# Layer 1's projections: the last two tiles' second gate cells move to the end of the query and key stage, and the stage's first tile is taken alone

## The chip, the cores and the metric

The kernel runs on one core of one Trainium2 chip. A core has a matrix engine (TensorE, PE in the profile), a vector engine (VectorE, DVE), an activation engine (ScalarE, ACT), a general engine (GpSimd, POOL) and a queue engine (SyncE, SP), which share an on-chip memory (SBUF) and the accumulator banks of TensorE (PSUM). Each engine works through its own list of instructions in order, and waits where an instruction needs something that another engine or a transfer has not yet delivered. Transfers (DMAs) are issued by an engine's queue and run beside it. The metric is the device time of one execution, in microseconds (us).

## The reference

The model is a stack of two layers over 2048 latent tokens and 256 context tokens with 1024 features each. Layer 0 is a mixture of full attention and gated linear attention; the change doesn't touch it. Layer 1 is a neighbourhood attention with 16 heads of 64 features. Cut to what matters:

```python
h  = rms_norm(x,  norm_g[1]) * (1 + scale)   + shift       # 2048 latent tokens
hc = rms_norm(cx, norm_g[1]) * (1 + c_scale) + c_shift     # 256 context tokens
q, k, v, z = jnp.split(jnp.dot(h, w_in), 4, axis=-1)       # 4 x 1024 columns, also for hc
q, k = rms_norm(heads(q), q_gain), rms_norm(heads(k), k_gain)
o = neighborhood_attention(q, k, v, k_ctx, v_ctx, rpb)     # window of 8 rows x 16 columns, and all 256 context keys
y = jnp.dot(o * silu(z), w_out)
x = x + gate * y
```

All of it is float32. The context's queries and gates are not needed in the last layer.

## The kernel before

The 2304 tokens are 18 tiles of 128: tiles 0 and 1 are the context, 2 to 17 the latent tokens. The 4096 columns of layer 1's input weights are eight blocks j of 512: 0 and 1 queries, 2 and 3 keys, 4 and 5 values, 6 and 7 gates. A "cell" (t, j) is one tile against one block. A float32 product is made as three products of split halves (high by high, high by low, low by high), so a cell is 24 matmuls of 128x512, eight steps of three (`mm3_steps`, L124 to L131). Tiles 0 and 1 have no query and gate cells.

Layer 1 has three stages.

`odd_qk` computes keys and queries, tile after tile. `cells` (L171 to L176) writes the order of the cells by hand: it takes the tiles in groups and goes through the blocks j within each group. The first two tiles form one group, the last two another, and those between are alone. `stream` (L178 to L195) turns that order into instructions. Two tiles can be held at once (`hbufs`, two buffers of `hhi` and `hlo`); once a tile's last cell is emitted, the tile two further on is prepared in its place. The preparation (`transposed`, `modulate`) loads the tile, sums its squares (ACT), scales it (DVE L328), transposes it on PE (L331, eight matmuls into `px`), evicts it through ACT with the layer's modulation, and splits it into high and low halves (DVE L343, L344). The weights of a block lie in one of four places w0 to w3, each with a high and a low half (`OD_PLACE`): blocks 2, 3, 0, 1 lie in w0, w1, w2, w3, and blocks 4, 5, 6, 7 follow in the same places. When the last cell of a block is through, the next block of its place is loaded over SP's queue (`wraw`, three buffers) and split on ACT (L106) and DVE (L383) in small steps, which `pump` hands out, one for every four steps of the matmuls.

A key or query cell is normalised per head (ACT square, DVE L1136, two small POOL operations, DVE L1139); then `fin` transposes it on PE (L1147, four matmuls), evicts it (ACT, into `oqh`, two buffers) and stores it: queries and keys over SP's queue (Q1, K1), a second arrangement of the keys over POOL's queue (K1t, L1184). `fin` of a cell is emitted while later cells run (`pend`). At the end of the stage the tiles 16 and 17 also get their first gate cells, j = 6: the gate is a tanh on ACT and a product on DVE (L1199), transposed like the others and stored to `z1` over POOL's queue (L1151).

`odd_vz` computes values and gates of all tiles, now from tile 17 down to tile 0, since tiles 16 and 17 are still held. Its first cells are written out by hand, and its gate cells go through their own transposes (L1239), an eviction into `ozt` and a store on ACT's queue (L1243). Woven between these cells runs `maxes`: for each of the 16 heads and 16 blocks of 128 queries, the maximum score that each query can meet, which needs two matmuls per block (L1273, L1280, into five banks `mx`) and reductions on DVE (L1275, L1286). `maxes` loads a key head pair (`mk`), a bias table per head (`mtab`, L1257) and the queries (`mq`, L1267) over SP's queue; POOL adds two masks to each table (L1258, L1259), ACT rearranges the queries into `mz`, whose unused halves DVE has set to zero (L1248). `weave` hands out 0.57 steps of `maxes` for each step of three matmuls, from the stage's first step, and lets a step of the cells be issued no earlier than a lag of 15 behind those maxima.

`odd_attention` follows. Its first loads (queries, keys, values, bias tables, masks, all at L111) are issued by SP's queue, and POOL adds a mask to its tables (L1370) ahead of the scores' correction on DVE (L1537).

The order in which each engine meets the instructions comes from the order of emission and from a scheduler that may take an instruction later than emitted, within its dependencies.

Of the kernel before, what the change touches and what calls it, by code (L numbers as in the profile page):

```python
# [10 lines left out]
F32 = mybir.dt.float32  # L11
# [6 lines left out]
P = 128  # L18
# [5 lines left out]
NT = T // P  # L24
NCT = CTX // P
# [63 lines left out]
class Kern:  # L89
# [79 lines left out]
                pass  # L169

    @staticmethod  # L171
    def cells(tiles, js, keep=lambda t, j: True, edge=2):

        n = len(tiles)
        groups = [tiles[:edge]] + [[t] for t in tiles[edge : n - edge]] + [tiles[n - edge :]]
        return [(t, j) for g in groups for j in js for t in g if keep(t, j)]  # L176

    def stream(self, cells, hT, cell, prep, done=None):  # L178
# [922 lines left out]
    def odd_qk(self, ws, win, hT):  # L1101
        nc = self.nc
# [6 lines left out]
        with ExitStack() as es:  # L1109
# [6 lines left out]
            pend, kt = [], {}  # L1116

            def cell(t, j):
                hi, lo = hT[t]
                wh, wl = win[j]  # L1120
                ps = self.tl(pp, [P, 8, 64], "gm", bufs=3)
                steps = self.mm3_steps(ps[:], (lambda k: hi[:, k, :], lambda k: lo[:, k, :]),
                                       (lambda k: wh[:, k, :], lambda k: wl[:, k, :]), range(KD))
                for n, _ in enumerate(steps):
                    if n == 5 and pend and (len(pend) > 1 or j == 6):
                        fin(*pend.pop(0))
                    yield
                if j == 6:
                    n = self.tl(sp, [P, 512], "onat", bufs=4)
                    self.gate(n, ps[:].rearrange("p h d -> p (h d)"))  # L1130
                    pend.append((t, j, n))
                    return
                sq = self.tl(sp, [P, 512], "osq")
                self.act(sq[:], ps[:].rearrange("p h d -> p (h d)"), AF.Square)
                ss = self.tl(sp, [P, 8], "oss", bufs=4)
                nc.vector.tensor_reduce(out=ss[:], in_=sq[:].rearrange("p (h d) -> p h d", h=8), axis=AX.X, op=ALU.add)  # L1136
                self.rpow(ss[:], ss[:], 1.0 / 64, EPS)
                n = self.tl(sp, [P, 512], "onat", bufs=4)
                nc.vector.tensor_tensor(out=n[:].rearrange("p (h d) -> p h d", h=8), in0=ps[:],  # L1139
                                        in1=ss[:].unsqueeze(2).to_broadcast([P, 8, 64]), op=ALU.mult)  # L1140
                pend.append((t, j, n))

            def fin(t, j, n):
                z = j // 2
                ps = self.tl(pp, [P, 4, P], "tp")
                for i in range(4):
                    nc.tensor.transpose(ps[:, i, :], n[:, i * P : i * P + P], self.ident[:])  # L1147
                hi = self.tl(sp, [P, 4, P], "oqh", F32R)
                if j == 6:
                    self.act(hi[:].bitcast(F32), ps[:])  # L1150
                    nc.gpsimd.dma_start(self.z1[:4, :, (t - NCT) * P : (t - NCT) * P + P].rearrange("j p t -> p j t"), hi[:].bitcast(F32))  # L1151
                    return
                self.act(hi[:], ps[:], AF.Copy, scale=qkg[:, z : z + 1])
                j0 = (j % 2) * 4
                if z == 1:
                    nc.sync.dma_start(self.K1[j0 : j0 + 4, :, t * P : t * P + P].rearrange("j p t -> p j t"), hi[:].bitcast(F32))
                if z == 0 or t < NCT:
                    lo = self.tl(sp, [P, 4, P], "oql", F32R)
                    nc.vector.scalar_tensor_tensor(out=lo[:], in0=ps[:], scalar=qkg[:, z : z + 1], in1=hi[:],
                                                   op0=ALU.mult, op1=ALU.subtract)  # L1160
                    if z == 0:
                        for part, tt in enumerate((hi, lo)):
                            nc.sync.dma_start(self.Q1[part][j0 : j0 + 4, :, (t - NCT) * P : (t - NCT) * P + P].rearrange("j p t -> p j t"),
                                              tt[:].bitcast(F32))
                    else:
                        store_k((hi, lo), j0, t * P, P)
                    return
                g, r0 = divmod(2 * (t - NCT), 8)
                if r0 == 0:
                    kt[j] = [self.tl(sp, [P, 4, 512], f"okt{j}{part}", F32R, bufs=1) for part in range(2)]  # L1170
                view = lambda x, n: x[:].rearrange("p i (r c b) -> p i r c b", r=n, c=4)
                for r in range(2):
                    oh, ol = (x[:].rearrange("p i (c b r) -> p i r c b", c=4, r=8)[:, :, r0 + r] for x in kt[j])
                    self.act(oh, view(ps, 2)[:, :, r], AF.Copy, scale=qkg[:, z : z + 1])
                    nc.vector.scalar_tensor_tensor(out=ol, in0=view(ps, 2)[:, :, r], scalar=qkg[:, z : z + 1],
                                                   in1=view(hi, 2)[:, :, r], op0=ALU.mult, op1=ALU.subtract)
                if r0 == 6:
                    store_k(kt.pop(j), j0, CTX + g * 512, 512)

            def store_k(parts, j0, o, w):  # L1180

                for u, x in enumerate(parts):
                    for i in range(2):
                        nc.gpsimd.dma_start(self.K1t[j0 : j0 + 4, i, u * 64 : u * 64 + 64, o : o + w].rearrange("j d t -> d j t"),  # L1184
                                            x[i * 64 : i * 64 + 64].bitcast(F32))

            nxt = {2: 4, 3: 5, 0: 6, 1: 7}
            done = lambda j: j in nxt and self.ahead.append(self.od_steps(win, nxt[j], ws))
            cells = self.cells(list(range(NT)), (2, 3, 0, 1), lambda t, j: j > 1 or t >= NCT)[:-8]
            cells += [(t, j) for j in (0, 1, 2, 3, 6) for t in (NT - 2, NT - 1)]  # L1190
            for _ in self.stream(cells, hT, cell, lambda t: self.prep(1, t, self.x1, pp, ("px", 2)), done):
                self.pump()
            while pend:
                fin(*pend.pop(0))
# [19 lines left out]
    def odd_vz(self, ws, win, hT):  # L1214
        nc = self.nc
        self.M1 = self.scr("M1", (16, SEQ), F32)
        NR, NC = (len(b) for b in BLOCKS["q"])
        with ExitStack() as es:
# [78 lines left out]
                        nc.gpsimd.dma_start(self.M1[h, g * 512 : g * 512 + 512].rearrange("(a c b) -> c a b", a=8, c=4),  # L1297
                                            r[4 * g : 4 * g + 4].rearrange("c (a b) -> c a b", a=8).bitcast(F32))

            cells = [(t, j) for j in (7, 4, 5) for t in (NT - 1, NT - 2)]  # L1300
            cells += self.cells(list(range(NT))[::-1], (4, 5, 6, 7), lambda t, j: j < 6 or t >= NCT)[8:]
            gemms = self.stream(cells, hT, cell, lambda t: self.reload(1, t))
            self.weave(gemms, maxes(), 0.57, 15)
# [395 lines left out]
```

## Time and profile before

| | |
|---|---|
| median of 3 runs | 3710.65 us (3707.5 to 3712.75) |
| the profiled execution's own time | 3709.59 us |
| its span, first to last instruction | 3707.8 us |
| mean granted clock of TensorE | 0.982 of full speed |
| TensorE busy | 3566.3 us, 96% |
| VectorE, ScalarE, GpSimd busy | 64%, 39%, 33% |
| query and key stage | about 2187 to 2626 us of the span |
| value and gate stage | about 2626 to 3114 us |

The profile is one execution. A row of a timeline gives an instruction's start and duration, its engine and line, the tiles it writes and reads, its shape, and in brackets how long the engine had stood idle before it and which instruction released it. A row of a window gives the length of the stretch, the busy time and number of instructions of PE, of its weight loads (PEld), DVE, ACT and POOL, the granted clock of TensorE, the share of the DMA engines' time in use, and the rate in GB/s. Matmuls are pipelined: a 128x512 matmul is shown with some 0.39 us, while the next one starts 0.23 us after it.

### The profile page before, as it was taken

How to read it: one execution, taken by the hardware profiler on the slowest of the kernel's cores; microseconds unless marked ns; L12 is line 12 of the kernel's file. 1: busy time of each engine (PE TensorE's matmuls, PEld its weight loads, DVE VectorE, ACT ScalarE, POOL GpSimd, SP SyncE). 2: the span in 40 equal slices, each digit the busy share in tenths (PEclk: the TensorE clock that was granted, in tenths of full speed). 3: DMA queues.
4: the chain of work that ended last, by engine and by line, in shares of the span. 5: the costliest groups of instructions: out<-in, count | busy, mean ns of one | idle time of the engine just before them, and what ended most of it. 6: DMA issues, size and time to landing. Idle time of an engine off the chain costs nothing.

```text
span 3707.8 us, 51752 instructions
## 1 busy us (share of the span) xinstructions
PE 3566.3 (96%) x18404; PEld 2754.6 (74%) x18404; DVE 2374.2 (64%) x4860; ACT 1438.5 (39%) x2741; POOL 1209.2 (33%) x1336
## 2 busy tenths in 40 slices
PE   7999989999999999999999999999899999999889
PEld 6988988888886666655656878888688887555567
DVE  4677656888876666697665344545478773666722
ACT  5545541111115555555553124444322223555400
POOL 1433420111111212122201233333344443777743
PEclk9999999999999999999999999999999999999999
DMA  7455453222242232334514543445744437887564
GB/s 257 138 164 160 129 170 98 87 75 85 75 127 63 82 97 79 91 105 121 163 55 151 165 149 117 150 142 175 215 143 123 136 117 200 216 215 205 162 195 130
DMA packets 364372, 512.18 MB, mean 138 GB/s; under 512 B 25826, under 2 KB 243890, under 8 KB 358211
## 3 DMA queue, kind: packets, MB, share of 16 engines
q1 hardware_dynamic: 322642, 425.49, 39.0%
q0 software_dynamic: 19872, 55.92, 5.1%
q10 hardware_dynamic: 21600, 27.46, 2.1%
q8 instruction: 146, 2.39, 0.3%
q14 instruction: 112, 0.91, 0.1%
HBM read 329.38 MB, written 179.37 MB: 137 GB/s over the span
## 4 chain that ended last, share of the span: by engine, by line
PE 79%; DVE 7%; DMA 6%; POOL 3%; ACT 3%; issue 2%; SPq 0%; POOLq 0%; ACTq 0%; DVEq 0%
PE gm L129 9%; PE gm L130 9%; PE gm L131 9%; PE av L905 7%; PE st L963 4%; PE mx L651 4%; PE st L964 3%; PE st L965 3%; PE pj L129 3%; PE pj L130 3%; PE pj L131 3%; PE o L1406 2%; PE st L1373 1%; DMA wraw<-w_od 1%; PE mx L1280 1%
## 5 line engine op out<-in xcount | busy, mean ns | idle before, releaser
L954 DVE TENSOR_TENSOR acc<-acc,apt 128x512 f32<-128x512 f32 x512 | 364.6, 737 | 158.3 <-ACT apt L106 155.4
L106 ACT ACTIVATE apt<-st 128x512 f32<-128x512 f32 (+1 forms) x592 | 344.4, 594 | 284.3 <-PE st L965 247.2
L652 DVE TENSOR_REDUCE mm<-mx 128x1 f32<-128x512 f32 (+1 forms) x656 | 389.3, 629 | 81.3 <-PE mx L651 74.4
L905 PE MATMUL av<-apt,av 128*64 128x512 f32 (+1 forms) x1184 | 288.0, 600 | 0.0
L963 PE MATMUL st<-aq,akh 97*128 97x512 f32 (+1 forms) x592 | 254.0, 429 | 5.1 <-ACT apt L106 2.8
L651 PE MATMUL mx<-mk,mq 96*128 96x512 f32 (+1 forms) x656 | 236.8, 373 | 6.1 <-DMA mq<-QT 4.6
L964 PE MATMUL st<-aq,akh 96*128 96x512 f32 (+1 forms) x592 | 235.2, 397 | 0.0
L965 PE MATMUL st<-aq,akl 96*128 96x512 f32 (+1 forms) x592 | 234.0, 396 | 0.0
L1286 DVE CUSTOM_DVE_ANT_1 mx<-mx,mtab 128x225 f32<-128x225 f32 (+12 forms) x576 | 183.7, 339 | 58.1 <-PE mx L1280 42.7
L106 ACT ACTIVATE u<-gm 128x352 f32<-128x352 f32 (+1 forms) x140 | 68.6, 497 | 369.4 <-PE gm L131 208.0
L905 PEld LDWEIGHTS av<-apt,av 128*64 128x64 f32 x1184 | 82.1, 138 | 157.1 <-issue 155.8
L1537 DVE TENSOR_TENSOR opt<-st,tab 128x64 f32<-128x64 f32 (+10 forms) x576 | 142.7, 316 | 86.6 <-PE st L1374 58.3
L963 PEld LDWEIGHTS st<-aq,akh 97*128 97x128 f32 x592 | 112.3, 190 | 98.4 <-issue 43.7
L1412 POOL TENSOR_TENSOR oacc<-oacc,opt 128x682 f32<-128x682 f32 (+9 forms) x144 | 169.6, 1206 | 23.2 <-ACT opt L106 21.9
L1073 POOL TENSOR_TENSOR px<-py,px 128x512 f32<-128x512 f32 x64 | 86.4, 1350 | 232.8 <-DVE py L1072 232.8
L106 ACT ACTIVATE opt<-opt 128x930 f32<-128x930 f32 (+8 forms) x130 | 104.4, 805 | 106.2 <-DVE opt L1537 102.3
L106 ACT ACTIVATE prh<-pr 128x1024 fp32r<-128x1024 f32 x32 | 33.9, 1058 | 263.1 <-PE pj L130 235.6
L651 PEld LDWEIGHTS mx<-mk,mq 96*128 96x128 f32 x656 | 121.7, 189 | 17.6 <-issue 5.0
L965 PEld LDWEIGHTS st<-aq,akl 96*128 96x128 f32 x592 | 113.6, 192 | 25.5
L964 PEld LDWEIGHTS st<-aq,akh 96*128 96x128 f32 x592 | 113.9, 192 | 18.0
L1373 PE MATMUL st<-q,kt 128*128 128x480 f32 (+5 forms) x256 | 99.0, 389 | 25.8 <-DVE opt L1537 20.9
L106 ACT ACTIVATE x<-px,modB,modA 128x128 f32<-128x128 f32 x272 | 99.3, 469 | 57.2 <-PE px L331 50.9
(517 smaller groups left out, 10069.0 us busy)
## 6 DMA issues: line engine op xcount, KB each, us to landing
q<-Q SPq DMA_DIRECT2D x48, 512.0 KB
H<-x ACTq DMA_DIRECT2D x36, 512.0 KB
adaw<-ada_w SPq DMA_DIRECT2D x64, 256.0 KB
x<-H SPq DMA_DIRECT2D x32, 512.0 KB
pr<-RT SPq DMA_DIRECT2D x32, 512.0 KB
wraw<-w_od SPq DMA_DIRECT2D x64, 256.0 KB
K1t<-okt POOLq DMA_DIRECT2D x32, 512.0 KB, 7.6
kt<-K1t SPq DMA_DIRECT2D x32, 512.0 KB
```

The source lines that it names most:

```text
L106: return self.nc.scalar.activation(out, in_, func, **kw)
L129: self.nc.tensor.matmul(out, lh(k), rh(k), start=j == 0, stop=False)
L130: self.nc.tensor.matmul(out, lh(k), rl(k), start=False, stop=False)
L131: yield self.nc.tensor.matmul(out, ll(k), rh(k), start=False, stop=j == n - 1)
L651: mm = nc.tensor.matmul(ps[:, :w], q[:A_QK, (t % 6) * P : (t % 6) * P + P], k[:A_QK, k0 : k0 + w], start=True, stop=True)
L652: nc.vector.tensor_reduce(out=m[:, t, n : n + 1], in_=ps[:, :w], axis=AX.X, op=ALU.max)
L905: nc.tensor.matmul(O[j, nb][i * 64 : i * 64 + 64, :w], V[j, kt // TT][:, kt % TT, i * 64 : i * 64 + 64], pts[i][:, :w], start=n == 0, stop ...
L954: nc.vector.tensor_tensor(out=acc[i][:, :w], in0=a[:, :w], in1=pts[i][:, :w], op=ALU.add)
L963: nc.tensor.matmul(ps[:, :w], kh[: A_QK + 1, i, kq], qh[: A_QK + 1, :w], start=True, stop=False)
L964: nc.tensor.matmul(ps[:, :w], kh[:A_QK, i, kq], ql[:A_QK, :w], start=False, stop=False)
L965: mm = nc.tensor.matmul(ps[:, :w], kl[:A_QK, i, kq], qh[:A_QK, :w], start=False, stop=True)
L1286: nc.vector.tensor_tensor_reduce(out=s, in0=s, in1=tb[:, ri : ri + rn, ci : ci + cn], scale=1.0, scalar=-3e38, op0=ALU.add, op1=ALU.max, a ...
```

## The change

`cells` gets a parameter `head`, the size of the first group of tiles; `odd_qk` calls it with 1, so that tile 0's two cells are taken ahead of tile 1's, where the two tiles' cells alternated. At the end of `odd_qk` the tiles 16 and 17 also get their second gate cells, j = 7; the conditions that meant the first gate cell now mean both, and the store's place in `z1` follows j. `odd_vz` no longer begins with these two cells.

```diff
-    def cells(tiles, js, keep=lambda t, j: True, edge=2):
+    def cells(tiles, js, keep=lambda t, j: True, head=2, edge=2):
 
         n = len(tiles)
-        groups = [tiles[:edge]] + [[t] for t in tiles[edge : n - edge]] + [tiles[n - edge :]]
+        groups = [tiles[:head]] + [[t] for t in tiles[head : n - edge]] + [tiles[n - edge :]]
         return [(t, j) for g in groups for j in js for t in g if keep(t, j)]
...
                 for n, _ in enumerate(steps):
-                    if n == 5 and pend and (len(pend) > 1 or j == 6):
+                    if n == 5 and pend and (len(pend) > 1 or j > 5):
                         fin(*pend.pop(0))
                     yield
-                if j == 6:
+                if j > 5:
                     n = self.tl(sp, [P, 512], "onat", bufs=4)
                     self.gate(n, ps[:].rearrange("p h d -> p (h d)"))
                     pend.append((t, j, n))
...
                 hi = self.tl(sp, [P, 4, P], "oqh", F32R)
-                if j == 6:
+                if j > 5:
                     self.act(hi[:].bitcast(F32), ps[:])
-                    nc.gpsimd.dma_start(self.z1[:4, :, (t - NCT) * P : (t - NCT) * P + P].rearrange("j p t -> p j t"), hi[:].bitcast(F32))
+                    nc.gpsimd.dma_start(self.z1[(j - 6) * 4 : (j - 6) * 4 + 4, :, (t - NCT) * P : (t - NCT) * P + P].rearrange("j p t -> p j t"), hi[:].bitcast(F32))
                     return
...
-            cells = self.cells(list(range(NT)), (2, 3, 0, 1), lambda t, j: j > 1 or t >= NCT)[:-8]
-            cells += [(t, j) for j in (0, 1, 2, 3, 6) for t in (NT - 2, NT - 1)]
+            cells = self.cells(list(range(NT)), (2, 3, 0, 1), lambda t, j: j > 1 or t >= NCT, 1)[:-8]
+            cells += [(t, j) for j in (0, 1, 2, 3, 6, 7) for t in (NT - 2, NT - 1)]
...
-            cells = [(t, j) for j in (7, 4, 5) for t in (NT - 1, NT - 2)]
+            cells = [(t, j) for j in (4, 5) for t in (NT - 1, NT - 2)]
             cells += self.cells(list(range(NT))[::-1], (4, 5, 6, 7), lambda t, j: j < 6 or t >= NCT)[8:]
```

The tail of `odd_qk` drops the last eight cells of the order that `cells` gives and writes those of tiles 16 and 17 out; `odd_vz` drops the first eight of its order in the same way.

## The prediction

> **What bounds the kernel now.** I read the page's totals and its chain first, then the windows around layer 1's query/key stage (2187 to 2626 us) and value/gate stage (2626 to 3114 us), then TensorE's timeline at the three places where it stands still, then the queues there.
>
> ```profile
> PE 3566.3 (96%) x18404; PEld 2754.6 (74%) x18404; DVE 2374.2 (64%) x4860; ACT 1438.5 (39%) x2741; POOL 1209.2 (33%) x1336
> PE 79%; DVE 7%; DMA 6%; POOL 3%; ACT 3%; issue 2%; SPq 0%; POOLq 0%; ACTq 0%; DVEq 0%
> ```
>
> TensorE (PE) is busy 96% of 3707.8 us. The change keeps every matmul, so it can only win back PE's holes and the half-clock time behind them. Windows (length, busy us of PE, PEld, DVE, ACT, POOL, granted clock, DMA share, GB/s):
>
> ```profile
> 2213.00:2215.00 2.00, 1.36 (x8) 0.96 (x8) 2.00 (x4) 1.44 (x5) 1.84 (x3) 0.80 0.84 228
> 2215.00:2221.00 6.00, 5.54 (x15) 4.46 (x16) 3.75 (x8) 2.69 (x8) 3.94 (x7) 0.50 1.01 322
> 2574.00:2580.00 6.00, 6.00 (x28) 4.91 (x27) 1.06 (x3) 0.00 (x0) 0.00 (x0) 1.00 0.46 175
> 2620.00:2640.00 20.00, 8.58 (x36) 6.32 (x34) 8.98 (x14) 10.77 (x18) 4.42 (x6) 0.77 0.77 230
> 2640.00:2660.00 20.00, 16.84 (x65) 13.56 (x66) 5.78 (x12) 5.00 (x9) 5.32 (x7) 0.84 0.97 320
> 2900.00:3000.00 100.00, 97.45 (x480) 81.63 (x479) 76.19 (x324) 25.10 (x41) 44.01 (x37) 1.00 0.43 136
> ```
>
> In the middle of the value/gate stage PE is at 97% with VectorE (DVE) at 76%: nothing to win there. The boundary at 2620 to 2660 has 14.6 us of PE idle, and clocks of 0.77 and 0.84. PE's timeline (start, duration, work, idle before and its releaser):
>
> ```profile
> 2213.51 1.36 PE L331 MATMUL px<-ident,x 128*128 128x128 f32 x8 [3.06 <-DVE x L328]
> 2215.46 1.09 PE L1147 MATMUL tp<-ident,onat 128*128 128x128 f32 x4 [0.59 <-DVE onat L1139]
> 2216.29 0.79 PE L129 MATMUL gm<-w0h,hhi 128*128 128x512 f32 x1
> 2572.76 0.50 PE L129 MATMUL gm<-w2h,hhi 128*128 128x512 f32 x1 [1.88 <-DVE hhi L343]
> ...
> 2625.97 0.40 PE L131 MATMUL gm<-w2h,hlo 128*128 128x512 f32 x1
> 2631.58 1.09 PE L1147 MATMUL tp<-ident,onat 128*128 128x128 f32 x4 [5.21 <-DVE onat L1139]
> ...
> 2640.47 1.11 PE L1147 MATMUL tp<-ident,onat 128*128 128x128 f32 x4 [6.47 <-ACT oqh L106]
> 2641.24 0.77 PE L129 MATMUL gm<-w3h,hhi 128*128 128x512 f32 x1
> ...
> 2653.26 0.39 PE L130 MATMUL gm<-w3l,hhi 128*128 128x512 f32 x1
> 2653.50 0.39 PE L131 MATMUL gm<-w3h,hlo 128*128 128x512 f32 x1
> 2656.57 0.66 PE L1239 MATMUL tp<-ident,ovz 128*128 128x128 f32 x4 [2.69 <-DVE ovz L1199]
> ...
> 2667.62 0.28 PE L1273 MATMUL mx<-mk,mz 128*128 128x256 f32 x1
> ```
>
> A matmul of 128x512 takes 0.23 us of pitch (2653.26 to 2653.50), a cell of 24 of them 5.5 us. From the last query/key matmul (2626.37) to the first maxima matmul (2667.62) pass 41.25 us. They hold 85 such matmuls (two cells of j=7 on w3, one of j=4 on w0, 13 of the next), 19.4 us, and five transpose groups of some 0.4 us net: about 21.5 us of work, so about 19.5 us are waits and slow clock.
>
> **The change, part by part.**
>
> *First tile alone.* Order now: (0,2),(1,2),(0,3),(1,3), then tile 2. Tile 0 frees its place only after three cells, and tile 2's preparation (square, scale, eight transposes, two splits) has one cell (5.5 us) as cover. Changed: (0,2),(0,3),(1,2),(1,3), two cells (11 us). No work is added. Preparation's steps now:
>
> ```profile
> 2206.18 1.05 ACT L106 ACTIVATE hlo<-x 128x1024 fp32r<-128x1024 f32 x1
> 2211.43 0.63 ACT L106 ACTIVATE w3h<-wraw 128x512 fp32r<-128x512 f32 x1 [0.38 <-DMA wraw<-w_od]
> 2212.71 0.75 DVE L328 TENSOR_SCALAR x<-x,ssx 128x1024 f32<-128x1024 f32 x1
> 2214.20 2.91 ACT L106 ACTIVATE x<-px,modB,modA 128x128 f32<-128x128 f32 x8 [0.56 <-PE px L331]
> ```
>
> The square (2206.18) moves six ACT instructions earlier, to about 2199.5; the scaling (2212.71, stuck behind w3l splits that wait for weights) to about 2204.5; the transposes run at about 2208.7 without a hole. But ACT's eight px evictions come in its order behind the w3h split of 2211.43, which waits for its DMA and doesn't move. From its end (2212.06), four evictions (half of 2.91, 1.5) and a cast of 0.4 give the first half of tile 2 at about 2214.0. PE, which carries the same work as before, gets there at about 2211.7. The two holes (3.65 us) become one of about 2.3 us, and tile 2's first matmul moves from 2216.29 to about 2214.1: **2.2 us** gained. Below: 0, if the weights' DMA releases that eviction later. Above: in 2215 to 2221 PE ran at 0.50, with 0.80 before it, a loss of 3.4 us; if the smaller hole no longer costs clock, the gain is 5.6. A hole of 1.88 us (2572.76) left the clock at 1.00; holes of 2.69 and 3.06 us lost it. 2.3 us lies between, in the middle; I count the clock as lost, since the row for the same place shows that. [...]
>
> *The last tiles' gate cells (16,7),(17,7) at the end of the query/key stage.* The edited conditions (j > 5) and the store's index cost nothing: they are evaluated while the program is built.
>
> ```profile
> 2607.95 0.69 DVE L383 TENSOR_TENSOR w3l<-wraw,w3h 128x512 fp32r<-128x512 f32 x1
> 2647.99 0.48 DVE L1248 MEMSET mz<- 64x512 f32 x1 [4.57 <-DMA z<-oqh]
> 2654.77 1.03 DVE L1248 MEMSET mz<- 64x512 f32 x2 [6.29 <-ACT ovz L106]
> ```
>
> The weights of these cells, w3, were split by 2608.6 (the last such row before the boundary), and their 48 matmuls need nothing else, so they slip into the holes. What goes from the value/gate stage: two tanh, two L1199, eight transposes, two evictions and two ACT-queue stores; the same work comes back on the query/key side, stores on POOL's queue. The first hole (5.21) stays: order on PE still puts transpose (17,3) ahead of the moved matmuls. From 2631.58 run, in order, 18 of w3, a transpose, 24, a transpose, 6, and the last two transposes: 48 matmuls at 0.23, some 1.9 us of half-clock loss as now, four transpose groups: last matmul at about 2646, gone is the wait of 6.47. The last gate's chain (tanh, L1199, transpose) is the one that now takes 2.69 us, its L1199 behind some 0.8 us of the memsets of 2654.77; without them I take 1.9 us. So w0's first matmul is at about 2648.5, where it now follows the transposes of 2656.57 at 2657.0. DVE's memset of mz, which waits for a gate store (4.57 us at 2647.99), will wait for the later ones; behind it on DVE stands nothing that is wanted before the first maxima. 70 matmuls on w0 and w1 stand ahead of the first maxima in the changed order (now 37): first maxima at about 2664.4, 34 PE instructions further on in the program: there the gain stands at some 3.2 + 34 x 0.23 = 11 us. Not all of it is kept.
>
> *The queues that the moved stores join.*
>
> ```profile
> 2640.71 0.81 POOL L1151 DMA_DIRECT2D z<-oqh  x1 [12.70 <-ACT oqh L106]
> ...
> 2658.74 3.20 POOL L1258 TENSOR_TENSOR mtab<-mtab,maskq 128x1798 f32<-128x1798 f32 x1 [13.64 <-DMA mtab<-rpb_q]
> 2669.57 7.36 POOL L1259 TENSOR_TENSOR mtab<-mtab,maskq 128x1798 f32<-128x1798 f32 x2
> 2650.43 0.33 SPq L1257 DMA_DIRECT2D mtab<-rpb_q  x1
> z<-oqh POOLq DMA_DIRECT2D x2, 256.0 KB, 8.6
> 2675.14 0.43 PE L1280 MATMUL mx<-mk,mz 128*128 128x360 f32 x1 [0.79 <-DVE mm L1275]
> 2676.74 0.49 PE L1280 MATMUL mx<-mk,mz 128*128 128x480 f32 x1 [0.47 <-DVE mm L1286]
> ```
>
> oqh has two buffers, and a POOL store takes 8.6 us to land. The four gate stores now stand on POOL's queue behind the last four key stores, so the evictions of (16,7) and (17,7) wait until the stores of (16,6) and (17,6) have landed, about 2653; the store of (16,7) then lands at about 2659. SP's first load of mtab reuses a place that now waits for that store: 2659 instead of 2650.43; mq, mz and the second mtab queue behind it. From there: 899 KB take 2.9 us at the 320 GB/s of the window 2640 to 2660, or the 8.3 us of now; POOL's mask adds 3.2 + 3.2 + 3.7: masks ready between 2672 and 2677.5, now 2673.25 (2669.57 and half of 7.36). I take 2675.3, the middle. PE waits about 1.2 us at the first maxima for mz, and, its five maxima banks full, some 2.6 us for the first L1286 on DVE, where it now lost 0.79 + 0.47. At 2678.2 PE stands 35 instructions further than now, less one more transpose group: **7.5 us** gained, of 4 (masks at 2677.5, or a further clock loss) to 9.5 (masks at 2672). Then PE at 97% carries it to the end of the stage: 3106.5 instead of 3114.
>
> *What comes next: the attention's loads.*
>
> ```profile
> 3077.13 1.97 SPq L111 DMA_DIRECT2D q<-Q  x3
> 3113.88 0.34 SPq L111 DMA_DIRECT2D maskk<-maskk  x1
> 3119.86 4.71 POOL L1370 TENSOR_TENSOR tab<-tab,maskk 128x1034 f32<-128x1034 f32 x2 [4.31 <-DMA maskk<-maskk]
> 3123.05 0.66 PE L1373 MATMUL st<-q,kt 128*128 128x384 f32 x1 [3.73 <-DVE opt L1537]
> 3077.00:3109.00 32.00, 32.00 (x146) 26.22 (x145) 3.95 (x12) 6.09 (x9) 7.33 (x12) 1.00 1.02 261
> 3122.00:3130.00 8.00, 6.40 (x20) 3.28 (x22) 5.51 (x25) 2.78 (x4) 5.98 (x5) 0.57 0.80 228
> ```
>
> These loads start when the last maxima matmul is through (3077.13), and hold the DMA at 1.02 for 32 us. The maxima are woven in at a fixed rate per matmul step from the stage's first step. With the stage two cells shorter, they end two cells nearer its end: 111 instructions, 25.4 us, ahead of it instead of 160, 36.6 us. So the last maxima come at 3106.5 - 25.4 = 3081, 4 us later than now, and the loads end at about 3113, when PE has been done with the stage for 6 us. The mask maskk now waits for the last cell's end (3113.88) and will wait behind those loads; POOL's add (3119.86), DVE's opt and PE's restart at 3123.05 follow. If the mask's load follows the stage's end, PE restarts 7.5 us earlier; if it follows the DMA's backlog (now empty at 3109, then at 3113, so about as late as 3113.88), hardly earlier. I take 3 us earlier of these 7.5, nearer the late end, because a DMA share of 1.02 leaves nothing to squeeze: **4.5 us** given back (0 to 7.5). The clock loss at 3122 to 3130 stays.
>
> **Sum.** 2.2 + 7.5 - 4.5 = 5.2 us less. Profiled execution: 3709.59 - 5.2 = 3704.4; it lies 1.06 us under the median of the runs (3710.65), which gives 3705.4: forecast 3705 us, -0.14%. The bound of what a measurement of this kernel tells from no change is 0.2%, 7.4 us.
>
> **Rivals.** (a) *The start keeps its clock*, the rest as forecast: 5.6 + 7.5 - 4.5 = 8.6 us less, 3702. For it: 1.88 us at 2572.76 cost none; against: 2.69 us did. [...] (b) *The attention's loads hide*: the mask lands right behind the stage's end, little is given back: 2.2 + 7.5 - 1 = 8.7 less, or with (a) 12 to 14: 3697 to 3702. For it: PE ran matmuls from 3114 to 3119 that need only loads issued early. Against: DMA at 1.02. (c) *Slower: the first mtab load*. The price is 1 us per us as soon as the masks come after about 2675. To lose 7.4 us net, that load must come 12.6 us later than 2659, at 2672, which needs the two store landings in a row to take 15 us instead of 8.6; then 3718. For it: POOL's first gate store already stood 12.70 us, and DMA was at 0.97. Against: two landings of 7 to 10 us now. (d) *Nothing*: the give-back takes all, 3710.
>
> **How the numbers follow.** Forecast 0.42 (its own range 3702 to 3709); (a) 0.16; (b) 0.24; (c) 0.13; (d) 0.05. Faster by over 0.2% = (a) + (b) = 0.40; within = forecast + (d) = 0.47; slower = 0.13. The range 3697 to 3714 reaches over (a), (b) and (d) and the milder half of (c), and leaves out the deepest of (b) with (a).
>
> **What would show it.** Right: px transposes near 2209 without idle; no 6.47 and 2.69 waits; w0's first matmul near 2648; mtab load near 2659; a PE hole under 4 us at the first L1286; last maxima about 25 us ahead of the stage's end; the attention's restart near 3120. Wrong: full clock behind the start's hole; mtab later than 2665; a restart at 3116 or after 3123.

## The result, and the profile after

The changed kernel takes 3728.8 us (median of 6 runs, 3723.1 to 3738.9), the kernel before in the same comparison 3711.7 us: 1.0047 times the time before, interval 1.0034 to 1.0060. It is slower by some 17 us; the forecast was 5 us faster. The profiled execution of the changed kernel took 3723.07 us, its span is 3721.3 us, at a mean clock of 0.980.

The page's totals and chain of the changed kernel:

```profile
PE 3573.3 (96%) x18404; PEld 2760.0 (74%) x18404; DVE 2386.6 (64%) x4860; ACT 1436.5 (39%) x2741; POOL 1208.7 (32%) x1338
PE 77%; DVE 8%; DMA 7%; ACT 3%; issue 3%; POOL 2%; SPq 0%; POOLq 0%; ACTq 0%; DVEq 0%
```

PE has the same 18404 instructions and 7 us more of busy time, which fits the slower clock in the windows below; the chain shows more of DVE and DMA. The totals don't tell where. PE's timeline does (start, duration, work, idle before and its releaser), with the holes, the stretches in which PE stands idle, at the places the prediction looked at:

```profile
2211.33 0.90 PE L1147 MATMUL tp<-ident,onat 128*128 128x128 f32 x3 [3.78 <-DVE onat L1139]
2230.10 1.03 PE L1147 MATMUL tp<-ident,onat 128*128 128x128 f32 x4 [4.72 <-DVE onat L1139]
...
2634.07 1.09 PE L1147 MATMUL tp<-ident,onat 128*128 128x128 f32 x4 [4.68 <-DVE onat L1139]
2650.67 0.66 PE L1147 MATMUL tp<-ident,onat 128*128 128x128 f32 x4 [0.97 <-DVE onat L1199]
2682.42 0.79 PE L131 MATMUL gm<-w0h,hlo 128*128 128x512 f32 x1 [7.32 <-DVE hlo L357]
3120.51 0.76 PE L1373 MATMUL st<-q,kc 128*128 128x512 f32 x1 [7.43 <-DMA q<-Q]
3131.47 0.66 PE L1373 MATMUL st<-q,kt 128*128 128x384 f32 x1 [0.93 <-DVE opt L1537]
```

The waits of 6.47 and 2.69 us at the boundary are gone, as the change meant them to go: 0.97 us is left of them. Three holes are new: 4.72 us at 2230, 7.32 us at 2682, 7.43 us at 3120. Behind each the granted clock is low besides, 0.50 to 0.57. The windows around them (length, busy us of PE, PEld, DVE, ACT, POOL, granted clock, DMA share, GB/s):

```profile
2211.00:2214.00 3.00, 2.67 (x9) 2.28 (x10) 2.59 (x6) 3.00 (x8) 0.39 (x1) 0.50 0.46 145
2230.00:2234.00 4.00, 3.90 (x12) 3.27 (x13) 2.58 (x4) 0.69 (x1) 4.00 (x4) 0.57 0.23 66
2675.00:2682.00 7.00, 0.10 (x1) 0.00 (x0) 7.00 (x1) 0.63 (x1) 6.25 (x4) 0.67 0.18 40
2682.00:2686.00 4.00, 3.58 (x8) 2.81 (x9) 1.93 (x12) 0.00 (x0) 0.00 (x0) 0.50 0.47 164
3113.00:3120.00 7.00, 0.07 (x1) 0.00 (x0) 0.00 (x0) 0.60 (x1) 0.54 (x1) 0.83 1.06 256
3120.00:3128.00 8.00, 7.24 (x16) 5.23 (x17) 2.53 (x3) 3.67 (x7) 0.00 (x0) 0.50 1.05 295
```

To see what is whose, I divided the time behind the even layer into stretches by PE's own marks: A from the first key matmul on w0 to the end of the last matmul of the gate cells j = 6; B from there to the last projection matmul; C from there to the attention's restart (the first `st<-q,kt` of 384 columns that waits for `opt`); D from there to the end of the span. All are differences of times in PE's timelines, in us. The table holds all kernels that were run; the second profile of each of the two kernels is there to show what chance does. Where a kernel below has lines of its own, the line numbers behind them stand two to seven higher (L1139 is L1144 in e7_order, L1258 is L1260 in e3_late).

| kernel | A | B | C | D | start of A to end |
|---|---|---|---|---|---|
| before | 439.0 | 487.5 | 9.1 | 584.8 | 1520.4 |
| before, second profile | 440.0 | 485.4 | 9.5 | 590.6 | 1525.5 |
| changed | 445.8 | 483.5 | 18.6 | 589.9 | 1537.7 |
| changed, second profile | 447.0 | 483.5 | 18.6 | 589.4 | 1538.5 |
| e1_head: first tile alone | 447.8 | 485.1 | 6.7 | 586.2 | 1525.9 |
| e2_gates: gate cells alone | 439.3 | 483.8 | 18.5 | 588.2 | 1529.9 |
| e3_late: changed, second table late | 447.8 | 474.1 | 18.2 | 593.3 | 1533.3 |
| e4_ratio: changed, maxima at 0.60 | 447.1 | 492.0 | 7.7 | 588.2 | 1535.1 |
| e5_g_late: gate cells, second table late | 438.6 | 473.3 | 18.5 | 594.2 | 1524.7 |
| e6_g_late_585: the same, maxima at 0.585 | 439.8 | 476.0 | 10.2 | 589.0 | 1515.0 |
| e7_order: first tile alone, orders mended | 439.5 | 484.3 | 7.6 | 589.4 | 1520.9 |
| e8_all: changed, all three repairs | 437.6 | 476.7 | 11.2 | 589.4 | 1514.9 |

Against the two profiles before, the changed kernel loses 6 to 8 us in A, wins 2 to 4 in B, loses 9 in C. D is work that the change doesn't touch; it differs by 6 us between two profiles of the same kernel before, so no difference in D is explained here. What lies ahead of A moves too: A starts between 2183.6 and 2192.7 us in these profiles. A, B and C together are some 13 us of the 17 that the medians differ by; where the rest lies is not shown.

### The profile page after: what moved, and what is told of

It reads as the page before. It is cut to its first block, busy times and chain, and to the rows that moved or that the text cites. A ratio compares the mean times of both kernels' runs of the same rounds, so it can differ in the third digit from the quotient of the medians.

```text
span 3721.3 us, 51753 instructions
## 1 busy us (share of the span) xinstructions
PE 3573.3 (96%) x18404; PEld 2760.0 (74%) x18404; DVE 2386.6 (64%) x4860; ACT 1436.5 (39%) x2741; POOL 1208.7 (32%) x1338
## 4 chain that ended last, share of the span: by engine, by line
PE 77%; DVE 8%; DMA 7%; ACT 3%; issue 3%; POOL 2%; SPq 0%; POOLq 0%; ACTq 0%; DVEq 0%
PE gm L129 8%; PE gm L130 8%; PE gm L131 8%; PE av L905 7%; PE st L963 4%; PE mx L651 4%; PE st L964 3%; PE st L965 3%; PE pj L129 3%; PE pj L131 3%; PE pj L130 3%; PE o L1406 2%; PE st L1373 2%; DMA wraw<-w_od 1%; PE o L1385 1%
## 5 line engine op out<-in xcount | busy, mean ns | idle before, releaser
L1286 DVE CUSTOM_DVE_ANT_1 mx<-mx,mtab 128x225 f32<-128x225 f32 (+11 forms) x576 | 183.8, 338 | 56.3 <-PE mx L1280 41.4
L1412 POOL TENSOR_TENSOR oacc<-oacc,opt 128x682 f32<-128x682 f32 (+10 forms) x144 | 169.6, 1198 | 23.3 <-ACT opt L106 22.0
L965 PEld LDWEIGHTS st<-aq,akl 96*128 96x128 f32 x592 | 113.6, 192 | 25.6
```

What stands on the lines that cost most here:

```text
L965: mm = nc.tensor.matmul(ps[:, :w], kl[:A_QK, i, kq], qh[:A_QK, :w], start=False, stop=True)
L1286: nc.vector.tensor_tensor_reduce(out=s, in0=s, in1=tb[:, ri : ri + rn, ci : ci + cn], scale=1.0, scalar=-3e38, op0=ALU.add, op1=ALU.max, a ...
```

## The loss at the start: two orders behind one load

The chain of the new hole at 2230, from the timelines of ACT, DVE and SP of the changed kernel:

```profile
2216.32 2.62 SPq L322 DMA_DIRECT2D x<-x  x1
2226.41 1.06 ACT L106 ACTIVATE hlo<-x 128x1024 fp32r<-128x1024 f32 x1 [11.52 <-DMA x<-x]
2227.47 1.06 ACT L106 ACTIVATE osq<-gm 128x512 f32<-128x512 f32 x2
2228.08 1.28 DVE L1136 TENSOR_REDUCE oss<-osq 128x8 f32<-128x512 f32 x2 [11.64 <-ACT osq L106]
2229.28 0.68 DVE L1139 TENSOR_TENSOR onat<-gm,oss 128x512 f32<-128x512 f32 x1
```

The transpose at 2230.10 needs the normalised cell of tile 1 (L1139 at 2229.28). Its factor had been ready since POOL finished at 2220.6, but on DVE it stands behind the two reductions of tile 2's key cells, those wait for ACT's squares of the same cells, and these stand on ACT behind the square of tile 3, which waits 11.52 us for tile 3's load. The kernel before, from its DVE and ACT timelines:

```profile
2220.96 0.69 DVE L1139 TENSOR_TENSOR onat<-gm,oss 128x512 f32<-128x512 f32 x1 [2.01 <-POOL oss L202]
2225.83 1.06 ACT L106 ACTIVATE hlo<-x 128x1024 fp32r<-128x1024 f32 x1 [8.14 <-DMA x<-x]
```

There the square of tile 3 waits for its load just so (8.14 us); but DVE has the normalisation ahead of those reductions, and PE comes to the place some 4 us later. Taking tile 0 alone changes both.

The first tile alone:

```diff
 # the kernel before, with
-    def cells(tiles, js, keep=lambda t, j: True, edge=2):
+    def cells(tiles, js, keep=lambda t, j: True, head=2, edge=2):
...
-            cells = self.cells(list(range(NT)), (2, 3, 0, 1), lambda t, j: j > 1 or t >= NCT)[:-8]
+            cells = self.cells(list(range(NT)), (2, 3, 0, 1), lambda t, j: j > 1 or t >= NCT, 1)[:-8]
```

> The kernel before with one part of the change: the first tile alone (head = 1), the gate cells where they were. Theory A (the loss of the start is this part's own): the wait of 4.7 us of PE for the normalised cell L1139, seen behind tile 2's key cells in the profile after, comes back with its half clock, because ACT's squares of tile 2's key cells stand behind the square of tile 3, which waits for its load; about 5 to 7 us slower than before, some 3718 us. Rival B (the loss of the start comes from the moved gate cells or from chance in the transfers): no such wait, and the time is that of before or the 2 us less that the prediction gave to this part, 3709 to 3712 us.

Measured: 3718.9 us against 3713.8, 1.0010 (1.0001 to 1.0018), so 4 to 5 us slower. The hole is there, PE's timeline and the window behind it:

```profile
2237.49 0.87 PE L1147 MATMUL tp<-ident,onat 128*128 128x128 f32 x3 [5.31 <-DVE onat L1139]
```

```profile
2238.00:2242.00 4.00, 4.00 (x12) 3.22 (x11) 2.48 (x4) 0.69 (x1) 4.00 (x4) 0.50 0.22 66
```

A is 447.8 us, as in the changed kernel. The loss of the start belongs to this part alone. Whether it is the two orders, the next kernel tells:

```diff
 # e1_head, with the preparation of tile 3 emitted two cells later, and
+        with self.tc.issue_after(self.lastsq.ins) if hasattr(self, "lastsq") and t == 3 else ExitStack():
             self.act(lo[:].rearrange("p k t -> p (k t)"), x[:], AF.Square, accum_out=ss[:, 0:1])
...
-                self.act(sq[:], ps[:].rearrange("p h d -> p (h d)"), AF.Square)
+                self.lastsq = self.act(sq[:], ps[:].rearrange("p h d -> p (h d)"), AF.Square)
...
+                with self.tc.issue_after(self.lastn.ins) if (t, j) == (2, 2) else ExitStack():
                     nc.vector.tensor_reduce(out=ss[:], in_=sq[:].rearrange("p (h d) -> p h d", h=8), axis=AX.X, op=ALU.add)
...
-                nc.vector.tensor_tensor(out=n[:]...
+                self.lastn = nc.vector.tensor_tensor(out=n[:]...
```

`issue_after` puts an instruction behind another one on the same engine.

> The first tile alone (the gate cells as before) with two orders fixed by hand: ACT's square of tile 3 behind the squares of tile 2's key cells, and DVE's first reduction of tile 2 behind the normalisation of tile 1's last cell. Theory A (the second hole of the start comes from these two orders): the wait of about 5 us behind tile 2's key cells goes, with its half clock; the query and key stage is 439 to 441 us long as before, not 446 to 448; 5 to 8 us less than with the first tile alone, the time of before. Rival B (the wait comes from the normalisation's own chain, or from the load of tile 3): a hole of over 3 us stays near the same place, and the stage stays at 445 or more.

Measured: 3712.9 us against 3715.6, 0.9996 (0.9985 to 1.0008), 5 to 6 us less than with the first tile alone. The two intervals overlap a little, but A does not: it is 439.5 us here, 437.6 to 440.0 in all seven profiles without this hole, and 445.8 to 447.8 in the five with it. The normalisation now runs ahead of the squares, and PE is busy throughout the stretch in which the hole was (DVE and ACT timelines, and a window):

```profile
2227.76 0.69 DVE L1144 TENSOR_TENSOR onat<-gm,oss 128x512 f32<-128x512 f32 x1 [4.24 <-POOL oss L205]
2229.22 0.60 ACT L106 ACTIVATE osq<-gm 128x512 f32<-128x512 f32 x1 [7.24 <-PE gm L131]
2233.02 1.06 ACT L106 ACTIVATE hlo<-x 128x1024 fp32r<-128x1024 f32 x1 [0.91 <-DMA x<-x]
```

```profile
2225.00:2235.00 10.00, 10.00 (x48) 8.23 (x47) 2.06 (x3) 2.92 (x5) 3.37 (x5) 1.00 0.58 169
```

So the 8 us between 447.8 and 439.5 are these two orders. The later preparation of tile 3, which the edit needs, does not explain them by an earlier load: the square of tile 3 starts 42.4 us after the start of A here, 42.2 in e1_head and 42.8 in the changed kernel. With the orders mended, the first tile alone neither wins nor loses measurably: its first hole (3.82 us at 2218 in this kernel) is as long as the one it replaces (3.06 and 0.59).

## The boundary: one DVE instruction of 12 us

At the boundary the change does what it says. But tile 15's reload (L357, low half of the split) takes twelve us, from the timelines of DVE and POOL of the changed kernel:

```profile
2670.39 11.97 DVE L357 TENSOR_TENSOR hlo<-x,hhi 128x1024 fp32r<-128x1024 f32 x1
2773.01 1.22 DVE L357 TENSOR_TENSOR hlo<-x,hhi 128x1024 fp32r<-128x1024 f32 x1 [0.64 <-ACT hhi L106]
2669.72 3.22 POOL L1258 TENSOR_TENSOR mtab<-mtab,maskq 128x1798 f32<-128x1798 f32 x1
2672.89 3.68 POOL L1259 TENSOR_TENSOR mtab<-mtab,maskq 128x1798 f32<-128x1798 f32 x1
2676.52 1.07 POOL L1212 DMA_DIRECT2D V<-ovz  x2
2677.61 3.66 POOL L1259 TENSOR_TENSOR mtab<-mtab,maskq 128x1798 f32<-128x1798 f32 x1
```

The same instruction takes 1.22 us at 2773. Here it starts 0.67 us after the second of POOL's four adds (2669.72) and ends 1.1 us after the last (2681.27): it is through only when POOL's row of three adds and two store issues is. The timeline shows the whole 11.97 us as busy time, with no idle in front. The trace shows who blocks: POOL's adds keep their 3.2 and 3.7 us; where an L357 comes first, at 2714.70, it takes 1.27 us, and the add that starts 0.26 us behind it takes 4.59. In this row L357 ends 1.1 us behind the last add, about the 1.22 us that it takes alone: as an estimate from these rows, it did next to nothing before POOL's row was through. Not all DVE work is held so: beside the add of 2714.96, L1199 (2715.89) took 0.67 us and L1275 (2716.49) 0.68, as L1275 did at 2683.25 with no add beside it. In the kernel before no L357 falls among these adds; the first one there is at 2680.98, 4 us behind the end of the last (2676.93):

```profile
2680.98 1.22 DVE L357 TENSOR_TENSOR hlo<-x,hhi 128x1024 fp32r<-128x1024 f32 x1
```

It is the change that brings the two together. Tile 15 takes tile 17's place, and without the two gate cells in front tile 17's last cell is the third of the stage instead of the fifth: counted from the end of A, this reload starts 14 us earlier (41.0 us instead of 54.6), while POOL's first add starts 4 us later (36.1 instead of 32.4).

Why the adds are late shows in SP's queue, which loads the tables: what it waited for from 2636 to 2662 (us in total, times, longest), first in the kernel before, then in the changed one, with the first table's load there.

```profile
SPq L1257 <- DMA K1t<-okt: 9.4, 2, 8.1
```

```profile
SPq L1223 <- DVE onat L1199: 9.4, 1, 9.4
2654.39 0.96 SPq L1257 DMA_DIRECT2D mtab<-rpb_q  x1
```

In the changed kernel the queue waits at the load of maskq (L1223) for the last gate cell's product, and issues the first table's load at 2654.39 (2650.43 before), ahead of the store of (16,7), which POOL issues at 2657.82. POOL's first add comes 11.1 us after that load (8.3 before).

The gate cells alone:

```diff
 # the changed kernel, with
-            cells = self.cells(list(range(NT)), (2, 3, 0, 1), lambda t, j: j > 1 or t >= NCT, 1)[:-8]
+            cells = self.cells(list(range(NT)), (2, 3, 0, 1), lambda t, j: j > 1 or t >= NCT)[:-8]
```

> The kernel before with the other part alone: the two gate cells moved, head = 2 as before. Theory A: the long DVE instruction L357 (12 us while POOL adds its masks) and the 7 us PE hole behind it come back, the value and gate stage ends about 4 us earlier than before relative to the query and key stage's end, and the attention opens with a wait for its loads; 5 to 12 us slower than before, 3717 to 3724 us. Rival B (the gate part is sound and the start alone costs): about 3 us faster than before as the prediction gave to this part, 3706 to 3710 us.

Measured: 3719.9 us against 3713.8, 1.0016 (1.0006 to 1.0026). L357 takes 11.50 us again, and PE's timeline has both holes:

```profile
2681.14 0.80 PE L131 MATMUL gm<-w0h,hlo 128*128 128x512 f32 x1 [7.38 <-DVE hlo L357]
3118.86 0.77 PE L1373 MATMUL st<-q,kc 128*128 128x512 f32 x1 [7.31 <-DMA q<-Q]
```

The gate part alone costs 6 us, with A as before; the theory of this run holds and its rival does not, though B won 2 to 4 us instead of the expected 4.

To take away what blocks L357, the second head's table is loaded later, so that POOL's second pair of adds comes after a pause:

```diff
 # the changed kernel, with
-                    nc.sync.dma_start(tb[:], self.i["rpb_q"][h].rearrange("p (r c) -> p r c", r=NR))
+                    with self.tc.issue_after(ql[2].ins) if h == 1 else ExitStack():
+                        nc.sync.dma_start(tb[:], self.i["rpb_q"][h].rearrange("p (r c) -> p r c", r=NR))
+                    ql = []
...
-                            nc.sync.dma_start(q[b : b + 64].bitcast(F32), self.Q1[0, j, b : b + 64, g * 512 : g * 512 + 512])
+                            ql.append(nc.sync.dma_start(q[b : b + 64].bitcast(F32), self.Q1[0, j, b : b + 64, g * 512 : g * 512 + 512]))
```

> The changed kernel with one edit: the load of the second head's bias table is queued on SP behind the first head's third query load, so that POOL's mask adds of the second head no longer follow those of the first without a gap. Theory A (DVE's L357 and POOL's mask adds shut each other out; L357 gets through only when POOL pauses): L357 starts where it did and is through at the end of the first head's second add, about 4 us instead of 12; the 7.3 us PE hole and its half clock go, the value and gate stage ends 7 to 9 us earlier, of which the attention's late loads take part back: 3 to 9 us less than the changed kernel, 3720 to 3726 us. Rival B (L357 was long for another reason, its input or a transfer): it stays at about 12 us and the time at 3729.

Measured: 3724.2 us against 3713.8, 1.0025 (1.0015 to 1.0036), about 5 us less than the changed kernel by the medians, 8 by the ratios. DVE and POOL timelines, and the window:

```profile
2674.97 2.84 DVE L357 TENSOR_TENSOR hlo<-x,hhi 128x1024 fp32r<-128x1024 f32 x1 [1.48 <-ACT hhi L106]
2672.97 3.75 POOL L1261 TENSOR_TENSOR mtab<-mtab,maskq 128x1798 f32<-128x1798 f32 x1
2679.84 3.20 POOL L1260 TENSOR_TENSOR mtab<-mtab,maskq 128x1798 f32<-128x1798 f32 x1 [2.12 <-DMA mtab<-rpb_q]
```

```profile
2660.00:2700.00 40.00, 38.86 (x178) 31.08 (x177) 22.03 (x88) 10.49 (x17) 21.62 (x18) 1.00 0.59 195
```

L357 ends 1.1 us after the one add that it meets (2676.72). PE's hole is gone, and B falls from 483.5 to 474.1 us: the boundary's gain over the kernel before is now 11 to 13 us, and the blocked instruction took 9.4 of them.

## The attention's opening: loads behind the last maxima

SP's queue of the changed kernel, and two rows of its waits over 3070 to 3135 (us in total, times, longest):

```profile
3087.32 1.72 SPq L111 DMA_DIRECT2D q<-Q  x3
3107.84 0.83 SPq L111 DMA_DIRECT2D tab<-rpb_k  x2
```

```profile
SPq L111 <- PE mx L1280: 16.6, 1, 16.6
SPq L111 <- DMA z<-ozt: 16.4, 2, 9.9
```

The first load comes at 3087.32, 25.6 us ahead of the stage's end at 3112.9 (3077.13 and 36.8 us before). This is what the prediction worked out: two cells less in the stage, and maxima handed out at the same rate from its start. Behind it the queue waits for stores of the last gate cells (`z<-ozt`), the rest of the loads comes in one go, and the DMA is at 1.06 while PE stands 7.43 us. To let the maxima end earlier, they are handed out faster:

```diff
 # the changed kernel, with
-            self.weave(gemms, maxes(), 0.57, 15)
+            self.weave(gemms, maxes(), 0.60, 15)
```

> The changed kernel with the maxima woven in at 0.60 steps for each matmul step instead of 0.57, so that they end about 20 us earlier against the end of the value and gate stage. Theory A (the attention's opening wait of 7.4 us comes from loads that start only behind the last maxima): that wait goes, the attention restarts 7 to 11 us earlier, about 3718 to 3722 us. Rival B (the opening waits for the gate stores and value stores of the last tiles, which come with the stage's end): the first loads are issued earlier but those behind the stores are not, the wait stays at over 4 us, and the time at 3726 to 3730.

Measured: 3725.2 us against 3713.8, 1.0033 (1.0020 to 1.0046). Neither expectation holds as written: the opening wait goes fully (C 7.7 instead of 18.6 us), but B grows from 483.5 to 492.0 us. A part of that is a new hole inside the stage, PE and ACT timelines:

```profile
3117.99 0.80 PE L129 MATMUL gm<-w1h,hhi 128*128 128x512 f32 x1 [3.29 <-ACT ovz L106]
3116.86 0.60 ACT L106 ACTIVATE ozt<-tp 128x512 f32<-128x512 f32 x1 [12.97 <-DMA z<-ozt]
```

The last maxima are 47.9 us ahead of the end, and the loads come early. ozt has one buffer, so ACT waits 12.97 us for a gate store to land (4.1 us in the changed kernel at this place, 7.3 before), and the last value cells wait for ACT. That the early loads crowd this store is likely, with the DMA share at 0.93 from 3100 to 3117, but not shown by a run. The hole with its slow clock (0.50 in the 2 us behind it) is, as an estimate from PE's rows, some 5 us of the 8.5; where the rest lies is open.

So neither rate is the best one. The next two kernels take the gate cells alone with the late table, at 0.57 and at 0.585, which puts the maxima's end 34.6 us ahead:

```diff
 # e2_gates with the edit of e3_late (e5_g_late); and, for e6_g_late_585,
-            self.weave(gemms, maxes(), 0.57, 15)
+            self.weave(gemms, maxes(), 0.585, 15)
```

> The kernel before with the gate cells moved (head = 2) and the second head's bias table loaded behind the first head's third query load: the changed kernel without its two costs at the start and at L357. Theory A (boundary gains, attention's opening takes part back): from the start of the query and key stage to the end of the value and gate stage 10 to 13 us less than before; the attention opens with a wait of 6 to 8 us for its loads, and restarts 2 to 4 us earlier than before; 3708 to 3712 us, against 3714 of before in the last comparison. Rival B (the end of the attention is held by something of its own, its loads or POOL): whatever the stages before it gain, the whole is within 1 us of before.

> The same with the maxima woven in at 0.585 instead of 0.57, which puts their end some 37 us ahead of the stage's end, as in the kernel before. Theory A: the opening wait goes too, the attention restarts 9 to 13 us earlier than before, 3700 to 3706 us. Rival B: the opening wait goes, but the denser maxima (or stores that the loads delay) cost as much inside the stage, as with 0.60: 3709 to 3715.

Measured, against 3715.6 us before: e5_g_late 3714.1 us, 0.9998 (0.9988 to 1.0009); e6_g_late_585 3706.5 us, 0.9980 (0.9971 to 0.9989). PE's timeline of the first, then of the second:

```profile
3111.53 0.76 PE L1375 MATMUL st<-q,kc 128*128 128x512 f32 x1 [7.44 <-DMA q<-Q]
```

```profile
3114.84 0.66 PE L1375 MATMUL st<-q,kt 128*128 128x384 f32 x1 [4.84 <-DVE opt L1539]
```

In e5_g_late the stages A and B are 14 us shorter than in the kernel before, and 9 of these are given back at the opening (C 18.5); the attention restarts 4.5 to 5.2 us earlier counted from the start of A, a little more than expected, but the time missed the expected 3708 to 3712 by 2 us, with the longest D of all (594.2). By its time alone this run says what rival B said, no gain within 1 us; the 5 us that the restart won are lost in D, for a cause that isn't shown. In e6_g_late_585 B gives back 2.7 us, C is 10.2, D is 589.0, and the whole is 0.2% faster than before, so an earlier restart does reach the end; it missed its upper end of 3706 by half a microsecond.

All three repairs on the changed kernel:

```diff
 # the changed kernel with the edits of e7_order and e3_late, and
-            self.weave(gemms, maxes(), 0.57, 15)
+            self.weave(gemms, maxes(), 0.585, 15)
```

> The changed kernel with all three repairs: the two orders at the start, the late second table, the maxima at 0.585. Theory A (the three places are the whole loss): the 17 us go and the boundary's gain stays: 3700 to 3708 us. Rival B (the parts interact, or the first tile alone costs even in the right order): 3709 or more, above the same without the first tile alone.

Measured: 3704.0 us against 3715.6, 0.9972 (0.9962 to 0.9983): 11.6 us faster than the kernel before, 25 to 28 us under the changed kernel. The three places account for the loss, and mended they leave the gain of the boundary. Of the opening it still has this (PE's timeline):

```profile
3118.16 0.66 PE L1380 MATMUL st<-q,kt 128*128 128x384 f32 x1 [5.84 <-DVE opt L1544]
```

It and e6_g_late_585 overlap in their intervals, so that the first tile alone adds anything is not shown.

Last, both kernels were profiled once more:

> The kernel before once more, for a second profile: how far the stages' lengths vary from one execution to the next. If the ledger of the stages is sound, the query and key stage is again 438 to 440 us, the value and gate stage from its first maxima 445 to 448, no wait at the attention's opening; the start of the stage and the attention behind its opening may move by some us.

> The changed kernel once more: the two holes of the start (3 to 4 and 4 to 6 us), the hole of 7 us behind an L357 of over 11 us, and the opening wait of 7 us are each there again, if they belong to the order of the instructions and not to chance; the query and key stage 445 to 448 us.

Measured: 3713.0 and 3730.3 us. The holes of the changed kernel came again, PE's timeline:

```profile
2235.10 0.66 PE L1147 MATMUL tp<-ident,onat 128*128 128x128 f32 x2 [4.91 <-DVE onat L1139]
2689.98 0.79 PE L131 MATMUL gm<-w0h,hlo 128*128 128x512 f32 x1 [7.40 <-DVE hlo L357]
3128.37 0.77 PE L1373 MATMUL st<-q,kc 128*128 128x512 f32 x1 [7.60 <-DMA q<-Q]
```

L357, which released the second of these, took 12.37 us. One expectation failed by a little: the first hole of the start was 2.74 us, not 3 to 4. The three new holes came in both profiles of the changed kernel, so they belong to the order of its instructions, not to chance.

## Why the prediction was wrong

The sum was 2.2 + 7.5 - 4.5 = 5.2 us less. In the profiles its three terms came out as a loss of 6 to 8 us, a gain of 2 to 4 and a loss of 9. The first two terms failed by the same step: the gain was counted on PE up to a point, and DVE and ACT were taken to be free there, while the new order had put other instructions in front. In the third the mechanism was right and the size was off.

- *First tile alone, 2.2 us gained.* Wrong in sign: A lost 6 to 8 us, and with that part alone the whole lost 4 to 5. The step up to tile 2's first matmul was about right in kind: it came 28.5 us after the stage's start instead of 28.9 (27.3 and 29.2 in the second profiles), so 0.4 to 1.9 us were gained. The hole that stayed was longer than the 2.3 us forecast (3.78, and 2.74 in the second profile) and was released by the normalised cell of L1139, not by the evictions the prediction named; on DVE that cell stood behind a split of w3, which waited for the weights. What failed is that the step ended there. The order on DVE and ACT behind tile 2's first matmul was not followed: there a cell of tile 1 had gone behind reductions of tile 2, and PE stood another 4.72 us.
- *Gate cells, first maxima at about 2664.4.* Near: first maxima 2667.2 with the stage 3 us late from its start (37.8 us behind the last j = 6 matmul; the forecast has 38.0). The waits of 6.47 and 2.69 us went; the hole in front of the transpose of (17,3) stayed at 4.68, as said. The tables were late, but not by the step that was forecast, a load of mtab at 2659 that waits for the landing of (16,7)'s store: the load came at 2654.39, ahead of that store, and took longer to land. That the first head's masks were ready at 2676.57, within 2672 to 2677.5 and near the 2675.3 forecast, is luck.
- *PE waits some 2.6 us for the first L1286, 7.5 us gained.* Wrong: a hole of 7.32 us, and B won 2 to 4 us. The term "first L1286" looked only at when the masks are ready, and took DVE as free by then; tile 15's reload, which the change moves among POOL's adds, was in none of its steps. Without the blocked L357 the gain is 11 to 13 us, more than the upper bound of 9.5.
- *The attention's loads, 4.5 us given back (0 to 7.5).* The mechanism was right and the size off: the loads begin 25.6 us ahead of the stage's end (25.4 forecast), but C grew by 9 us. The forecast had PE's matmuls on early loads run on, as before; here the first of them stood 7.43 us for `q<-Q`, a wait the prediction had no row for, and the tables stood behind gate stores.
- *The rivals.* (a), that the start keeps its clock, was wrong: 0.50 and 0.57 behind the two holes. (b), that the loads hide, was wrong. (c), slower through a late first table at the price of 1 us per us, named the right sign and the wrong mechanism: POOL's first add was late by 4 us counted from the end of A, and in e3_late, where it is as late (36.3 us), B wins 11 to 13 us all the same. Its condition, a load of mtab at 2672 behind two slow store landings, didn't come. The two orders at the start and the blocked L357 were in no rival; the opening was in the forecast, at half its size.
- *The clock.* It was counted as lost behind the start's hole, and was (0.50 from 2211 to 2214). In the twelve profiles the holes of 3.06 to 3.37 us lost the clock too (0.50 to 0.81 in the 2 us behind them). But the prediction's reading that 2.69 us loses it doesn't hold each time: behind that hole the clock was 0.79 in the 2 us, and behind the same hole at the boundary, 2.68 us in the second profile of the kernel before, 1.00.

## What to carry to other kernels

A step that comes earlier changes what stands next to it on every in-order engine: follow the new order on each until the first wait in it, and past the place where the gain is counted. L357 took 1.22 us with no add beside it and 11.97 us in POOL's row of adds: a DVE instruction like it can't be priced without POOL's row at the same time; before a cell is moved, look what heavy POOL work its DVE instructions will now meet. And where side work is woven in at a fixed rate, shortening the main stage moves its end towards the end of the stage: the rate has to be set anew, neither too late for what follows nor so early that its transfers may crowd the stage's own.

## What was not expected of the hardware

DVE's L357 was held through three POOL adds and the two store issues between them, 11.97 us for 1.22 us of work, and 11.50 to 12.37 us in the three other profiles that have this row of adds; with one add in front it took 2.4 to 2.8 us. In POOL's row it ended 1.1 us behind the last add.

The clock behind one and the same hole was not the same each time. In the twelve profiles, the windows of 2 us, from 0.2 us behind the end of each hole over 1.3 us between 2186 and 3130 us, show: behind holes of 3.0 us and more, the clock was under 0.85 each time; behind the hole of 1.87 us in the middle of stage A, which every kernel has alike, it was 1.00 in six profiles and 0.70 to 0.84 in six. So with holes under 3 us the length alone doesn't tell the clock behind it in these profiles. In the attention it is alike with holes of about 1 us: in the kernel before the hole of 1.04 us at 3184.07 is followed by 4 us at a clock of 1.00, in its second profile the same hole, 1.02 us at 3182.31, by 4 us at 0.59. This may be a part of the spread in D; that was not tested.
